# First norm's modulation in two halves of the channels; later modulation, constants and the context's projections moved

## The chip, the core and the metric

The kernel runs on one core of a Trainium2 chip. The metric is the device time of one execution in microseconds (us), as the median of three runs. The core has five engines that work side by side, each through its own instructions in order: TensorE (PE: matmuls and transposes), VectorE (DVE), ScalarE (ACT), GpSimd (POOL) and SyncE (SP), whose work here is to issue DMA transfers.

## What is computed

One call runs a hybrid block and then two layers of a second block, on 512 tokens of width 1024 with a context of 256 tokens. This case touches only the front of the first block:

```python
mod = silu(c) @ w_mod + b_mod            # 6 x 1024: shift, scale, gate, shift, scale, gate
hx  = rms_norm(x, g_mix) * (1 + scale) + shift
hc  = rms_norm(ctx, g_mix) * (1 + scale_c) + shift_c
px  = split_columns(hx @ w_in)           # q, k, v, gate of retention, windows, neighbourhoods
pc  = hc @ w_in[:, the k and v columns]  # the context's keys and values
ya  = retention_mixer(px, pc, log_sigmoid(decay_logit), ...)
mx  = gated_merge(px['gates'], ya, yb, yc, ...)
```

`c` and the context's `c_ctx` give two rows of modulation each time. After the merge come a mixture of 16 experts and the second block, whose two layers have modulations `mod_w[l]` of their own.

## The kernel before

Activations stay on chip with the channels on the partitions: `hx` is eight pairs of tiles of 128 channels x 512 tokens, `hc` the same with 256 tokens. A float32 product is made of three matmuls: `mm3` (L404 to L406) multiplies high by high, low by high and high by low part, and `w` loads a 512 KB weight piece through SP's queue (L412) and splits it on ScalarE (L395) and VectorE (L391). One projection is 24 matmuls: 8 tiles of channels x 3.

A modulation is `modblock` (L471): pieces of 128 x 1024 weights (512 KB, L470) come through SP's queue, and each gives two matmuls with the two silu columns as stationary operand, written to two groups of 32 rows. Then ScalarE copies the rows (L477), PE transposes them (L480), VectorE adds the bias. `modblock` is a generator that stops after each piece, and `pace`, `alt` and `weave` set how often the surrounding code takes one. For the block at hand:

- `block1_mixer` first drains the whole shift and scale modulation (`wmod0`, 16 pieces, seven buffers), computes `A1` from the scales, and norms all eight channel tiles (`normmod`, L569) to `hx`.
- Then it runs the first half of the retention's projections, `ret_proj(0)`: two q and two k projections with their rotation, the context's keys `kc`, the values `v`, the context's values `vc`, two gates. Between them `pace` takes pieces of the remaining modulations from the chain `mods` (`wmod1`, `wmod2`, then 24 pieces of the second block's layer 1, three buffers). `PACE` holds how much work lies between pieces.
- `ret_consts` (L734 on) computes the decay tables from the log-sigmoid; `ret_attn(0)` is woven with `ret_proj(1)` and `mods`, `ret_attn(1)` with output gates and `mods`; what is left of `mods` is then drained.
- Much later the third `merge` and `outproj` are alternated with the modulation of layer 0 of the second block (24 pieces, six buffers), one piece after each step of the merge and two after each step of `outproj`.

The text above sets priorities; a list scheduler then orders the instructions of each engine, and gives out buffers as they come free. Constants are loaded by `const` when first named, on GpSimd's queue.

## Time and profile before

| | |
|---|---|
| three runs | 2779.96, 2788.20, 2794.11 us; median 2788.20 |
| the profiled execution's own time | 2794.44 us |
| its span | 2792.6 us |
| mean granted clock of TensorE | 0.973 of 2.4 GHz |
| busy share of PE, DVE, ACT, POOL | 94%, 56%, 44%, 6% |
| bytes moved | 537.68 MB, mean 193 GB/s |

The span runs from the first to the last instruction; the time lies 1.8 us around it. A busy share is a mean over the whole span. The granted clock is the share of full clock that TensorE was given in a stretch: 1.00 is 2.4 GHz, 0.50 is 1.2 GHz. DMA share is the mean busy share of the core's 16 DMA engines.

### The profile page before, as it was taken

To read this page: it belongs to the slowest core of one execution; us is meant where nothing else is said; L and a number is where in the kernel's file an instruction comes from. 1 tells how busy PE (TensorE), PEld (TensorE's weight loads), DVE (VectorE), ACT (ScalarE), POOL (GpSimd) and SP (SyncE) were. 2 spreads that over 40 slices of the span, in tenths; PEclk is the share of its full clock that TensorE was granted. 3 is DMA by queue.
4 is the path that set the end of the run, shared out by engine and by line. 5 is a ranking of instruction groups with operands and counts; after the bars stand their busy time and mean duration, and the time that the engine had idled before them with its cause. 6 is when DMAs were issued, how large, how long until landed. Compare 5 with 4: busy or idle time off the path is not lost. (4 is left out here: it accounts for less than half of the span.)

```text
span 2792.6 us, 41759 instructions
## 1 busy us (share of the span) xinstructions
PE 2625.3 (94%) x16372; PEld 1859.9 (67%) x16372; DVE 1569.8 (56%) x2957; ACT 1230.6 (44%) x2159; POOL 161.0 (6%) x260
## 2 busy tenths in 40 slices
PE   6999999999958999999998899999999999999997
PEld 2666677887633566555654577777777777777776
DVE  3564677676441324456232656656866546766974
ACT  3333355444222224365222444545655645555652
POOL 1000001110001000000000000000010000000001
PEclk9899999999979999999999899999999999999998
DMA  8545424634879999988999332213354332114353
GB/s 287 177 164 191 146 85 161 209 120 156 298 283 325 340 380 356 335 297 300 352 366 372 126 106 83 77 51 136 118 186 135 128 123 84 62 39 140 117 177 114
DMA packets 167974, 537.68 MB, mean 193 GB/s; under 512 B 21272, under 2 KB 22376, under 8 KB 167776
## 3 DMA queue, kind: packets, MB, share of 16 engines
q1 hardware_dynamic: 138528, 460.40, 47.2%
q0 software_dynamic: 17152, 52.57, 5.8%
q10 hardware_dynamic: 12096, 22.03, 2.1%
q8 instruction: 129, 2.11, 0.3%
q14 instruction: 69, 0.57, 0.1%
HBM read 484.06 MB, written 48.76 MB: 191 GB/s over the span
## 5 line engine op out<-in xcount | busy, mean ns | idle before, releaser
L391 DVE TENSOR_TENSOR wl<-wr,wh 128x1024 fp32r<-128x1024 f32 x320 | 390.8, 1223 | 386.8 <-ACT wh L395 357.3
L395 ACT CAST wh<-wr 128x1024 fp32r<-128x1024 f32 x320 | 334.4, 1047 | 458.2 <-PE ps L405 348.6
L404 PE MATMUL ps<-hx,wh 128*128 128x512 f32 x1168 | 473.8, 406 | 5.8 <-ACT hx L569 5.1
L405 PE MATMUL ps<-hx,wh 128*128 128x512 f32 x1168 | 468.8, 402 | 0.1
L406 PE MATMUL ps<-hx,wl 128*128 128x512 f32 x1168 | 466.9, 400 | 0.0
L404 PEld LDWEIGHTS ps<-hx,wh 128*128 128x128 f32 x1168 | 221.8, 190 | 66.9 <-issue 13.2
L1307 PE MATMUL ps<-we,xe 128*64 128x512 f32 x1024 | 241.1, 615 | 18.1 <-DMA we<-in_wexp 18.0
L405 PEld LDWEIGHTS ps<-hx,wh 128*128 128x128 f32 x1168 | 221.6, 190 | 52.3 <-issue 8.4
L406 PEld LDWEIGHTS ps<-hx,wl 128*128 128x128 f32 x1168 | 221.7, 190 | 50.2 <-issue 3.3
L673 ACT ACTIVATE P<-ps,st 128x768 f32<-128x768 f32 (+3 forms) x144 | 111.1, 771 | 142.6 <-DVE st L669 107.7
L1307 PEld LDWEIGHTS ps<-we,xe 128*64 128x64 f32 x1024 | 76.0, 141 | 144.8 <-issue 118.4
L404 PE MATMUL ps<-hc,wh 128*128 128x256 f32 x496 | 144.1, 291 | 0.1
L406 PE MATMUL ps<-hc,wl 128*128 128x256 f32 x496 | 139.8, 282 | 0.5 <-DVE wl L391 0.5
L405 PE MATMUL ps<-hc,wh 128*128 128x256 f32 x496 | 140.3, 283 | 0.0
L667 DVE TENSOR_REDUCE st<-ps 128x1 f32<-128x768 f32 (+3 forms) x144 | 114.2, 793 | 38.1 <-PE ps L406 35.3
L1307 PE MATMUL ps<-we,hT 128*64 128x512 f32 x512 | 122.8, 626 | 10.4 <-DMA we<-in_wexp 8.2
L695 PE MATMUL ps<-c_ident,P 128*128 128x128 f32 x688 | 110.0, 278 | 5.3 <-ACT PT L698 3.5
L404 PEld LDWEIGHTS ps<-hc,wh 128*128 128x128 f32 x496 | 94.1, 190 | 19.5 <-issue 14.2
L695 PEld LDWEIGHTS ps<-c_ident,P 128*128 128x128 f32 x688 | 79.9, 140 | 39.8 <-ACT PT L698 13.4
L471 PE MATMUL ps<-wm,sc_cc 128*32 128x512 f32 x384 | 89.4, 647 | 15.9 <-DMA wm<-in_wmod 14.1
L698 ACT COPY PT<-ps 128x512 f32<-128x512 f32 x123 | 70.1, 586 | 72.6 <-PE ps L695 71.9
L405 PEld LDWEIGHTS ps<-hc,wh 128*128 128x128 f32 x496 | 94.0, 190 | 4.0 <-issue 3.5
(517 smaller groups left out, 5036.1 us busy)
## 6 DMA issues: line engine op xcount, KB each, us to landing
we<-in_wexp SPq DMA_DIRECT2D x384, 512.0 KB
wr<-in_win SPq DMA_DIRECT2D x240, 512.0 KB
wm<-in_wmod SPq DMA_DIRECT2D x48, 512.0 KB
wr<-in_wbr SPq DMA_DIRECT2D x48, 512.0 KB
dram<-th ACTq DMA_DIRECT2D x72, 256.0 KB
mth<-dram SPq DMA_DIRECT2D x72, 256.0 KB
wr<-in_wout SPq DMA_DIRECT2D x32, 512.0 KB
dram<-mth POOLq DMA_DIRECT2D x48, 256.0 KB, 3.1
```

The lines of the kernel that those rows point to most:

```text
L391: s.nc.vector.tensor_tensor(out, a, b, ALU.subtract)
L395: i = s.nc.scalar.copy(hi, src)
L404: t.matmul(out, a[0], b[0], start=start, stop=False)
L405: t.matmul(out, a[0], b[1], start=False, stop=False)
L406: t.matmul(out, a[1], b[0], start=False, stop=stop)
L471: nc.tensor.matmul(ps[32 * j:32 * j + 32, :], sc[:, k, :], w[:, j % 2 * 512:j % 2 * 512 + 512], start=k == 0, stop=k == 7)
L667: nc.vector.tensor_reduce(st[:, 0:1], sc[:, :n], AX.X, ALU.max)
L673: nc.scalar.activation(p[:, :n], sc[:, :n], AF.Exp, bias=st[:, 1:2], scale=scale, accum_out=st[:, 2:3])
L695: nc.tensor.transpose(tp[:, j:j + 128], blocks[(i + j) // 128], s.const("ident"))
L698: nc.scalar.copy(parts[i // 512][:, :m], tp[:, :m])
L1307: nc.tensor.matmul(ps[64 * e:64 * e + 64, :], stat[:, k, 64 * e:64 * e + 64], ws[h][e][:, kk * 512:kk * 512 + 512], start=k == 0, stop=k == 7)
```

## The change

Six things change. The host puts the columns of the shift and scale weights in another order, so that each of two blocks of 1024 columns holds shift and scale of four channel tiles. `block1_mixer` runs one modulation and one norm per half, with `x` multiplied by its reciprocal root mean square ahead of both. `modblock` takes its pieces in pairs: two transfers issued, the second piece's first, then four matmuls, then one stop. The chain `mods` is no longer taken between the first four projections nor, by the program's text, in the rest of `ret_proj(0)`; `PACE` is (0, 3.5, 3.5), and `outproj` takes one pair per step. In `ret_proj` the context's keys and values come last. Five constants, 576 KB in all, are loaded when the windows' stage begins.

```diff
+    half = np.concatenate([np.arange(s, s + 512) for s in (0, 1024, 512, 1536)])
+    wm, bm = f["w_mod"][0], f["b_mod"][0]
+    for n, a in enumerate(_modchunks(wm[:, half[:1024]]) + _modchunks(wm[:, half[1024:]]) + _modchunks(wm[:, 2048:])):
...
-    o["bmod"] = _cols(f["b_mod"][0])
+    o["bmod"] = _cols(np.concatenate([bm[half], bm[2048:]]))
...
+    def const(s, name, late=False):
+            i = s.nc.gpsimd.dma_start(t, a)
+            if late:
+                s.late(i)
...
-        for k in range(8):
-            for j in range(nj):
-                if j % 2 == 0:
-                    w = s.wp.tile([128, 1024], F32, name=s.uid("wr"), tag="wraw", bufs=NRAW) if big is None else \
-                        big.tile([128, 1024], F32, name=s.uid("wm"), tag="wbig", bufs=s.nbig)
-                    nc.sync.dma_start(w, src[k][:, j * 512:j * 512 + 1024])
-                nc.tensor.matmul(ps[32 * j:32 * j + 32, :], sc[:, k, :], w[:, j % 2 * 512:j % 2 * 512 + 512],
-                                 start=k == 0, stop=k == 7)
-                if j % 2:
-                    yield 0.9
+        parts = [(k, j) for k in range(8) for j in range(0, nj, 2)]
+        for i in range(0, len(parts), 2):
+            ws = []
+            for k, j in parts[i:i + 2][::-1]:
+                w = big.tile([128, 1024], F32, name=s.uid("wm"), tag="wbig", bufs=s.nbig)
+                nc.sync.dma_start(w, src[k][:, j * 512:j * 512 + 1024])
+                ws.insert(0, w)
+            for (k, j), w in zip(parts[i:i + 2], ws):
+                for e in range(2):
+                    nc.tensor.matmul(ps[32 * (j + e):32 * (j + e) + 32, :], sc[:, k, :], w[:, e * 512:e * 512 + 512],
+                                     start=k == 0, stop=k == 7)
+            yield 1.8
...
+    def normmod_x(s, x, k, a, b):
+
+        nc = s.nc
+        h = s.T(nm="nf")
+        nc.vector.tensor_scalar(h, x, a, b, ALU.mult, ALU.add)
+        hi, lo = s.TT(512, "hx", "hx")
+        nc.scalar.activation(hi, x, AF.Identity, bias=b, scale=a)
+        s.sub(lo, h, hi.bitcast(F32))
+        return hi, lo
...
-        for j in range(2):
-            kt = s.T(F32R, "kc", "pj")
-            ps = s.proj(win[c0 + 2 + j], s.hc, 256)
-            kc.append(s.split(ps[:, :256], kt[:, :256], kt[:, 256:]))
-            yield 2.6
...
-        yield from s.vproj(src, s.hc, 256, put(vc, "vc"))
         for j in range(2):
             gs.append(s.gate_silu(s.proj(win[c0 + 6 + j], s.hx), 512))
             yield 5.2
+        for j in range(2):
+            kt = s.T(F32R, "kc", "pj")
+            ps = s.proj(win[c0 + 2 + j], s.hc, 256)
+            kc.append(s.split(ps[:, :256], kt[:, :256], kt[:, 256:]))
+            yield 2.6
+        yield from s.vproj(src, s.hc, 256, put(vc, "vc"))
...
         rx = s.rstd_sb(s.sqsum(x, 512), D, 512)
+        for k in range(8):
+            nc.vector.tensor_tensor(x[k], x[k], rx, ALU.mult)
+        A1, B1 = [s.cp.tile([128, 2, 8], F32, name=n) for n in ("A1", "B1")]
+        s.hx = []
         with s.pool("bigA") as big:
             s.nbig = 7
-            drain(s.modblock(sc, s.d["wmod0"], 2048, mod, bm, 0, big))
-        A1 = s.cp.tile([128, 2, 8], F32, name="A1")
-        for v in range(2):
-            nc.vector.scalar_tensor_tensor(A1[:, v, :], mod[:, v, 8:16], 1.0, s.const("gmix"), ALU.add, ALU.mult)
-        s.hx = s.normmod(x, 512, A1[:, 0, :], mod[:, 0, 0:8], lambda: s.TT(512, "hx", "hx"), rx)
+            for hf in range(2):
+                c, o = 8 * hf, slice(4 * hf, 4 * hf + 4)
+                drain(s.modblock(sc, s.d[f"wmod{hf}"], 1024, mod, bm, c, big))
+                nc.vector.scalar_tensor_tensor(A1[:, :, o], mod[:, :, c + 4:c + 8], 1.0, gm2[:, :, o], ALU.add, ALU.mult)
+                nc.vector.tensor_copy(B1[:, :, o], mod[:, :, c:c + 4])
+                for k in range(4 * hf, 4 * hf + 4):
+                    s.hx.append(s.normmod_x(x[k], k, A1[:, 0, k:k + 1], B1[:, 0, k:k + 1]))
...
-            mods = itertools.chain(s.modblock(sc, s.d["wmod1"], 2048, mod, bm, 16, mr, bk[0]),
-                                   s.modblock(sc, s.d["wmod2"], 2048, mod, bm, 32, mr, bk[1]),
+            mods = itertools.chain(s.modblock(sc, s.d["wmod2"], 2048, mod, bm, 16, mr, bk[0]),
+                                   s.modblock(sc, s.d["wmod3"], 2048, mod, bm, 32, mr, bk[1]),
...
-                next(mods)
-            s.hc = s.normmod(c, 256, A1[:, 1, :], mod[:, 1, 0:8], lambda: s.TT(256, "hc", "hc"), rc)
-            drain(pace(g, mods, PACE[0]))
+            s.hc = s.normmod(c, 256, A1[:, 1, :], B1[:, 1, :], lambda: s.TT(256, "hc", "hc"), rc)
+            drain(g)
...
+            for n in ("ropem", "wrt", "cum", "pedge512", "pedge256"):
+                s.const(n, True)
...
-        drain(alt(s.outproj(hl, s.d["wout"], 512, put), mods, 2))
+        drain(alt(s.outproj(hl, s.d["wout"], 512, put), mods, 1))
...
-PACE = (2, 2.5, 2.5)
+PACE = (0, 3.5, 3.5)
```

`sub` of `normmod_x` is a subtraction on VectorE; in it ScalarE writes the high part and VectorE the shifted value and the low part.

How the instructions of PE move is seen at three places. `ps` are sums in PSUM, `wm` modulation pieces, `hx` and `hc` the normed inputs, `wh` and `wl` the two parts of a split weight piece, `qk` rotated queries and keys; the number is the buffer's in the program.

First place: PE between the first modulation and the first projection. Before:

```order
L471 MATMUL ps_153<-wm_210,sc_cc 32x512 x2
L471 MATMUL ps_153<-wm_214,sc_cc 32x512 x2
L480 MATMUL ps_220<-c_ident,mrow_218 128x128 x4
L404 MATMUL ps_302<-hx_235,wh_298 128x512
L404 MATMUL ps_375<-hx_235,wh_371 128x512
L405 MATMUL ps_302<-hx_236,wh_298 128x512
L405 MATMUL ps_375<-hx_236,wh_371 128x512
L471 MATMUL ps_289<-wm_411,sc_cc 32x512 x2
L471 MATMUL ps_289<-wm_457,sc_cc 32x512 x2
```

There two projections (`ps_302`, `ps_375`) begin behind the last transposes, and pieces of the next modulation follow. After, the end of the second half's pieces and what follows:

```order
L478 MATMUL ps_236<-wm_263,sc_cc 32x512 x2
L478 MATMUL ps_236<-wm_261,sc_cc 32x512 x2
L408 MATMUL ps_326<-hx_214,wh_322 128x512
L409 MATMUL ps_326<-hx_215,wh_322 128x512
L486 MATMUL ps_271<-c_ident,mrow_269 128x64 x4
L410 MATMUL ps_326<-hx_214,wl_323 128x512
L408 MATMUL ps_326<-hx_220,wh_322 128x512
L409 MATMUL ps_326<-hx_221,wh_322 128x512
L410 MATMUL ps_326<-hx_220,wl_323 128x512
```

Before, the whole modulation and its transposes (L480) stand ahead of the first projection matmul. After, the first half's transposes (L486, not shown) stand ahead of the second half's eight pieces, and the second half's transposes stand behind the first two projection matmuls; the projection's first twelve matmuls use the first half's channels.

Second place: PE behind the fourth projection (`ps_467` before, `ps_483` after). Before:

```order
L406 MATMUL ps_467<-hx_277,wl_464 128x512
L471 MATMUL ps_289<-wm_646,sc_cc 32x512
L471 MATMUL ps_289<-wm_689,sc_cc 32x512 x2
L471 MATMUL ps_289<-wm_719,sc_cc 32x512 x2
L497 MATMUL ps_515<-ones,sq_346 128x1 x2
L471 MATMUL ps_289<-wm_723,sc_cc 32x512 x2
L533 MATMUL ps_521<-c_ident,rs_518 128x128 x2
L471 MATMUL ps_289<-wm_754,sc_cc 32x512 x2
L471 MATMUL ps_289<-wm_784,sc_cc 32x512 x2
L471 MATMUL ps_289<-wm_827,sc_cc 32x512 x2
L471 MATMUL ps_289<-wm_831,sc_cc 32x512 x2
L404 MATMUL ps_581<-hc_528,wh_577 128x256
```

Here modulation pieces and the context's norm fill PE's queue up to the context's keys (`ps_581`). After:

```order
L408 MATMUL ps_483<-hx_300,wh_479 128x512
L409 MATMUL ps_483<-hx_301,wh_479 128x512
L410 MATMUL ps_483<-hx_300,wl_480 128x512
L478 MATMUL ps_313<-wm_1024,sc_cc 32x512
L408 MATMUL ps_598<-wh_588,hx_214 128x256
L409 MATMUL ps_598<-wl_589,hx_214 128x256
L410 MATMUL ps_598<-wh_588,hx_215 128x256
```

Before, seven and a half pieces and the context's norm (L497, L533) stand between the fourth projection and the next; in all, sixteen stand in `ret_proj(0)`. After, half a piece stands here, four and a half in `ret_proj(0)`, and the next rows are those of the values `v` (`ps_598`), with the context's last. Four pieces stand in a row behind the first score matmuls that follow:

```order
L408 MATMUL ps_1015<-qk_358,qk_431 128x512
L409 MATMUL ps_1015<-qk_359,qk_431 128x512
L410 MATMUL ps_1015<-qk_358,qk_432 128x512
L478 MATMUL ps_313<-wm_1152,sc_cc 32x512
L478 MATMUL ps_313<-wm_1150,sc_cc 32x512 x2
L478 MATMUL ps_313<-wm_1160,sc_cc 32x512 x2
L478 MATMUL ps_313<-wm_1158,sc_cc 32x512 x2
L849 MATMUL ps_966<-A_971,v_623 128x512
L408 MATMUL ps_1036<-hx_214,wh_1032 128x512
```

Behind them is the first product with the decay tables (`A_971`). None of these pieces stood here before: their matmuls moved down the queue from the projections.

Third place: the end of the 24 pieces of layer 1. Before:

```order
L471 MATMUL ps_289<-wm_2151,sc_cc_511 32x512 x2
L471 MATMUL ps_289<-wm_2155,sc_cc_511 32x512 x2
L471 MATMUL ps_289<-wm_2159,sc_cc_511 32x512 x2
L406 MATMUL ps_2220<-hx_247,wl_2217 128x512
L404 MATMUL ps_2220<-hx_253,wh_2216 128x512
L405 MATMUL ps_2220<-hx_254,wh_2216 128x512
L406 MATMUL ps_2220<-hx_253,wl_2217 128x512
L404 MATMUL ps_2220<-hx_259,wh_2216 128x512
L405 MATMUL ps_2220<-hx_260,wh_2216 128x512
L406 MATMUL ps_2220<-hx_259,wl_2217 128x512
L404 MATMUL ps_2220<-hx_265,wh_2216 128x512
L471 MATMUL ps_289<-wm_2163,sc_cc_511 32x512 x2
```

Three pieces stand together, then one at a time among projection matmuls. After:

```order
L478 MATMUL ps_313<-wm_2151,sc_cc_523 32x512 x2
L478 MATMUL ps_313<-wm_2149,sc_cc_523 32x512 x2
L486 MATMUL ps_2159<-c_ident,mrow_2157 128x128 x4
L478 MATMUL ps_313<-wm_2177,sc_cc_523 32x512 x2
L478 MATMUL ps_313<-wm_2175,sc_cc_523 32x512 x2
L478 MATMUL ps_313<-wm_2185,sc_cc_523 32x512 x2
L478 MATMUL ps_313<-wm_2183,sc_cc_523 32x512 x2
L478 MATMUL ps_313<-wm_2193,sc_cc_523 32x512 x2
L478 MATMUL ps_313<-wm_2191,sc_cc_523 32x512 x2
L478 MATMUL ps_313<-wm_2201,sc_cc_523 32x512 x2
L478 MATMUL ps_313<-wm_2199,sc_cc_523 32x512 x2
L486 MATMUL ps_2209<-c_ident,mrow_2207 128x64 x4
```

Before, five of the last eight pieces stand one by one among projection matmuls. After, the last eight, in four pairs, follow each other and the transposes with no other matmul between.

## Rows read from the trace of the kernel before

**Rows 1.** Windows: us, busy PE, PEld, DVE, ACT, POOL, PEclk, DMA share, GB/s

```profile
16.00:38.26 22.26, 17.23 (x69) 2.99 (x67) 0.35 (x2) 1.26 (x4) 2.84 (x6) 1.00 1.01 377
...
75.90:93.40 17.50, 10.87 (x38) 2.15 (x37) 16.43 (x35) 8.22 (x16) 0.00 (x0) 0.64 0.69 241
93.40:133.75 40.35, 40.35 (x256) 34.65 (x257) 13.56 (x34) 11.34 (x20) 0.00 (x0) 0.95 0.42 141
```

**Rows 2.** Timeline of PE, 36 to 134 us: start, us, instruction [idle before, releaser]

```profile
36.52 1.05 PE L471 MATMUL ps<-wm,sc_cc 128*32 128x512 f32 x4 [0.23 <-DMA wm<-in_wmod]
...
40.99 0.49 PE L404 MATMUL ps<-hx,wh 128*128 128x512 f32 x1 [2.07 <-ACT hx L569]
...
133.52 0.39 PE L406 MATMUL ps<-hx,wl 128*128 128x512 f32 x1
```

**Rows 3.** Waits of PE, 0 to 120 us: total us, times, longest

```profile
PE ps L471 <- DMA wm<-in_wmod: 13.9, 16, 2.6
```

**Rows 4.** Waits of PE, 120 to 460 us

```profile
PE ps L471 <- DMA wm<-in_mw1b: 1.8, 2, 1.3
```

**Rows 5.** Timeline of PE, projections of 512 and of 256 columns

```profile
57.22 0.39 PE L404 MATMUL ps<-hx,wh 128*128 128x512 f32 x1
...
59.49 0.39 PE L405 MATMUL ps<-hx,wh 128*128 128x512 f32 x1
...
98.11 0.28 PE L404 MATMUL ps<-hc,wh 128*128 128x256 f32 x1
...
98.71 0.40 PE L405 MATMUL ps<-hc,wh 128*128 128x256 f32 x2
```

**Rows 6.** Timeline of PE, pieces among the merge's and outproj's matmuls

```profile
698.09 0.39 PE L406 MATMUL ps<-yn,wl 128*128 128x512 f32 x1
698.41 1.05 PE L471 MATMUL ps<-wm,sc_cc 128*32 128x512 f32 x4
699.39 0.50 PE L404 MATMUL ps<-yn,wh 128*128 128x512 f32 x1
...
702.34 1.05 PE L471 MATMUL ps<-wm,sc_cc 128*32 128x512 f32 x4
...
732.60 1.07 PE L471 MATMUL ps<-wm,sc_cc 128*32 128x512 f32 x8
```

**Rows 7.** Timelines of SP's queue and of PE: pieces from issue to use

```profile
44.61 2.73 SPq L470 DMA_DIRECT2D wm<-in_wmod  x3
...
296.52 0.33 SPq L470 DMA_DIRECT2D wm<-in_mw1b  x1
...
48.33 1.05 PE L471 MATMUL ps<-wm,sc_cc 128*32 128x512 f32 x4 [1.36 <-DMA wm<-in_wmod]
...
300.66 1.05 PE L471 MATMUL ps<-wm,sc_cc 128*32 128x512 f32 x4 [0.41 <-DMA wm<-in_mw1b]
...
303.95 1.05 PE L471 MATMUL ps<-wm,sc_cc 128*32 128x512 f32 x4 [1.35 <-DMA wm<-in_mw1b]
```

**Rows 8.** Timeline of PE and a window: waits and the clock behind them

```profile
876.11 6.13 PE L1307 MATMUL ps<-we,hT 128*64 128x512 f32 x20 [4.14 <-DMA we<-in_wexp]
...
876.00:879.50 3.50, 3.39 (x8) 1.00 (x10) 0.00 (x0) 0.00 (x0) 0.00 (x0) 0.51 0.12 48
...
91.44 1.92 PE L471 MATMUL ps<-wm,sc_cc 128*32 128x512 f32 x4 [1.99 <-DMA wm<-in_wmod]
```

**Rows 9.** Timeline of ACT, then DVE's first product with the decay (summary of L832)

```profile
128.73 0.21 ACT L734 ACTIVATE ls<-c_lgt 128x8 f32<-128x8 f32 x1
...
L832 DVE SCALAR_TENSOR_TENSOR A<-ps,G x8: 628/685/694, 139.7 to 190.0; 128x512 f32<-128x512 f32 x8
```

**Rows 10.** Windows of the merge and the output projection

```profile
680.00:698.00 18.00, 18.00 (x99) 14.42 (x98) 4.82 (x7) 6.67 (x12) 0.00 (x0) 1.00 0.80 289
698.00:730.00 32.00, 32.00 (x132) 18.98 (x131) 19.61 (x27) 8.87 (x12) 2.12 (x4) 1.00 0.90 306
730.00:760.00 30.00, 30.00 (x144) 20.47 (x143) 11.57 (x13) 7.36 (x9) 2.17 (x4) 1.00 0.90 325
```

More of the change, by code (lines that the diff above doesn't have):

```diff
@@ L149, in prep @@
     o["cc"] = np.ascontiguousarray(np.stack([_cols(f["c"][0]), _cols(f["c_ctx"])], axis=-1))
-    m = _modchunks(f["w_mod"][0])
-    for n, a in enumerate(m):
+    half = np.concatenate([np.arange(s, s + 512) for s in (0, 1024, 512, 1536)])
+    wm, bm = f["w_mod"][0], f["b_mod"][0]
+    for n, a in enumerate(_modchunks(wm[:, half[:1024]]) + _modchunks(wm[:, half[1024:]]) + _modchunks(wm[:, 2048:])):
         o[f"wmod{n}"] = a
-    o["bmod"] = _cols(f["b_mod"][0])
+    o["bmod"] = _cols(np.concatenate([bm[half], bm[2048:]]))
     o["gmix"] = _cols(f["g_mix"][0])
@@ L368, in sc @@
         return s.P1("sc", 1536)
-    def const(s, name):
+    def const(s, name, late=False):
         if name not in s.cache:
@@ L373, in const @@
             t = s.cp.tile(list(a.shape), a.dtype, name="c_" + name)
-            s.load(t, a)
+            i = s.nc.gpsimd.dma_start(t, a)
+            if late:
+                s.late(i)
             s.cache[name] = t
@@ L1095, in block1_mixer @@
         bm = s.const("bmod")
+        gm2 = s.cp.tile([128, 2, 8], F32, name="gm2")
+        for v in range(2):
+            nc.vector.tensor_copy(gm2[:, v, :], s.const("gmix"))
         x = s.loadx("xT", 512, "pj")
         rx = s.rstd_sb(s.sqsum(x, 512), D, 512)
+        for k in range(8):
+            nc.vector.tensor_tensor(x[k], x[k], rx, ALU.mult)
+        A1, B1 = [s.cp.tile([128, 2, 8], F32, name=n) for n in ("A1", "B1")]
+        s.hx = []
         with s.pool("bigA") as big:
             s.nbig = 7
-            drain(s.modblock(sc, s.d["wmod0"], 2048, mod, bm, 0, big))
-        A1 = s.cp.tile([128, 2, 8], F32, name="A1")
-        for v in range(2):
-            nc.vector.scalar_tensor_tensor(A1[:, v, :], mod[:, v, 8:16], 1.0, s.const("gmix"), ALU.add, ALU.mult)
-        s.hx = s.normmod(x, 512, A1[:, 0, :], mod[:, 0, 0:8], lambda: s.TT(512, "hx", "hx"), rx)
+            for hf in range(2):
[5 more added lines that the diff above has]
+                    s.hx.append(s.normmod_x(x[k], k, A1[:, 0, k:k + 1], B1[:, 0, k:k + 1]))
         md, gd = s.dram([8, 128, 512]), s.dram([24, 128, 512])
```

## Prediction

> **What bounds the kernel now.** I read the page's busy shares first: TensorE (PE) is busy for 94% of the span, so a change pays where PE waits or where its clock is halved, and hardly elsewhere. The share is a mean over stages, so I went on to the windows. Three stretches matter [rows 1]. From 16.0 to 38.3 us the DMA share is 1.01 at 377 GB/s: the first modulation streams its sixteen 512 KB pieces as fast as they come, and PE follows it. From 75.9 to 93.4 us PE is busy for only 10.87 of 17.50 us at a mean clock of 0.64. From 93.4 to 133.75 us PE is busy throughout. Then the timeline of PE [rows 2]: the first modulation's last piece ends at 36.52 + 1.05 = 37.57 us, the first projection matmul starts at 40.99 us, and the last matmul of the first retention projections starts at 133.52 us and ends its stretch at 133.75 us. So this front part takes 133.75 - 37.57 = 96.2 us. The list of PE's waits up to 120 us puts 13.9 us on modulation pieces still in flight [rows 3], and from 120 to 460 us only 1.8 us on the last ones [rows 4]. What the front costs without waits follows from two steady intervals [rows 5]: ten 512-column matmuls between 57.22 and 59.49 us give 0.227 us each, five 256-column ones between 98.11 and 98.71 us give 0.12 us each.
>
> **The change part by part.** All sums are made against the profiled execution, 2794.4 us (span 2792.6 and 1.8 us around it); it lies 6.2 us above the median of the three runs, 2788.2.
>
> *Front.* By the code and the order there are 144 matmuls of 512 columns and 192 of 256 columns in the first retention projections: 144 x 0.227 + 192 x 0.12 = 32.7 + 23.0 = 55.7 us. Before, sixteen later modulation pieces stood among them; after, four and a half. A piece put into a stream of projections costs what lies between the projection matmul ahead of it and the one behind, less that one's own interval: 699.39 - 698.09 - 0.23 = 1.07 us, with a slower restart 1.2 us [rows 6]. A group of eight modulation matmuls (two pieces on different columns) has the same busy time, 1.07 against 1.05 us [rows 6]. Two and a half pairs and their restarts: 4 us, with other small work 6 us. For the start I take 3 us: the first half's norm is done while the second half's pieces stream, so the first matmul no longer waits for hx, but the second half's norm has only the first half's twelve matmuls (12 x 0.227 = 2.7 us) as cover, and a short dip of the clock may follow. 55.7 + 6 + 3 = 64.7 us, so the front loses 96.2 - 64.7 = 31.5 us (28 to 34). What is late next there is PE itself. The halves do not bring the first modulation's end forward: the same sixteen pieces still come at the DMA's rate, its last pair runs 1.05 us longer because its last-landing piece is needed first, and the deferred constants (576 KB, 0.59 MB) free 0.59 MB at 377 GB/s = 1.6 us. I count these at nothing. Deferred, the constants go down GpSimd's queue much later, where DMA has room; a gain or loss of 1.6 us is the bound.
>
> *New waits of PE for pieces.* Pieces are now taken in pairs, but still from three buffers, and SyncE (SP) issues its queue in order. By the buffers' release, the piece of a pair that PE needs first goes into the buffer which the pair before it frees with its own first piece. So its transfer can't start before PE has done that one, and PE must have other work for as long as the transfer takes. The trace has two pieces that PE waited for, from issue to use: 296.52 to 300.66 us, 4.14 us, and 44.61 (the first of three issues) to 48.33 us, 3.72 us [rows 7]. I take 3.9 us. In most places projections of 5 us and more stand between pairs. Not so in four: after the first score matmuls, where two pairs stand together (3.7 us of wait, which also hides the late decay chain, below); one pair at the ends of the second modulation's pieces (3.0); the last pair but four (1.8); and the final four pairs of the 1024-wide modulation, which now run with nothing in between (the last order above). There the first of the four has its neighbour's second piece and four transposes as cover, 3.9 - 1.0 - 0.7 = 2.2 us of wait; the three others only a second piece, 3.9 - 0.85 = 3.05 us each; and the transposes at the end wait some 0.8 us for ScalarE's copy: 2.2 + 9.2 + 0.8 = 12.2 us. Sum of waits: 3.7 + 3.0 + 1.8 + 12.2 = 20.7 us; the 2.0 us of such waits that stood in this stretch go (1.8 of them in [rows 4]), so +18.7 us (12 to 22). Behind these waiting matmuls stand the second retention and the later projections on PE, and nothing passes them. The pieces that left the front are run here too, but as pairs they cost per pair about what a single cost: +0.6 us.
>
> *Clock.* In this trace a wait of 4.14 us before 876.11 us is followed by 3.5 us at 0.51 [rows 8], 1.7 us lost; and behind a wait of 1.99 us at 91.44 us, one of several in a row, four modulation matmuls took 1.92 us [rows 8] in place of 1.05, the clock's lower level, 1.2 instead of 2.4 GHz. I charge 1.7 us for each of the two waits of 3 us and more, and for the final four pairs 4 x (1.92 - 1.05) + about 2.5 us behind them = 6 us: +9.4 us (0 to 11). On the Trainium skill, page "TensorE: Matmul & The Clock Gate", section "HAM oscillation — how this bites in real kernels": it warns that short bursts of matmuls, each waiting for its own transfer, keep falling back to the low clock. It speaks against this change, and the row at 91.44 us agrees; without it the clock term would be nothing, with it as here.
>
> *Decay chain.* ScalarE's first step is at 128.73 us and the first product with it at 139.7 us [rows 9], 11 us, before under gates and scores. It now starts after the context's projections, which come last; about 8 us of score and projection matmuls cover it, the rest falls into the 3.7 us above. Alone it would cost 3 us; beside that wait nothing.
>
> *Merge.* The third merge and output projection now take pieces in pairs, so sixteen groups of matmuls (eight single pieces, then eight pairs) become twelve: -4 x 1.2 = -4.8 us. But the merge now needs sixteen pieces where it took eight: 8 x 0.52 MB at 377 GB/s = 11.1 us more of DMA in stretches whose shares are 0.80, 0.90 and 0.90 [rows 10]. Up to 730 us that leaves 18 x 0.20 + 32 x 0.10 = 6.8 us free; up to 4.3 us could show as waits. Six buffers hold three pairs ahead, so I take 2 us (0 to 7, and more with the clock, see the third rival): -2.8 us (-5 to +6).
>
> Sum: -31.5 + 18.7 + 0.6 + 9.4 - 2.8 = -5.6 us. From 2794.4 that is 2788.8, and with the profile's 6.2 us over the median taken off, 2782.6; I say 2783.
>
> **The rivals.** *First: the waits are short and the clock stays up.* For it: a piece that streams is 0.52 MB at 377 GB/s = 1.4 us in the first modulation [rows 1], and single waits of 1 to 2 us in the trace (1.35 at 303.95 [rows 7]) left the clock alone. Against it: a buffer's release, an issue and a landing follow each other here, none streaming. If a transfer takes 2.6 us, each of about seven chained waits is 1.3 us shorter: waits +10.3, clock +2: -31.5 + 10.3 + 0.6 + 2 - 2.8 = -21.4 us, 2767 us. The Trainium skill, page "DMA: Bandwidth & Descriptors", section "Anatomy of one DMA — SWDGE (gpsimd) path", gives about 2.0 us and the bytes at 436 GB/s, by estimate 3.2 us for a piece; by it the seven waits would be some 5 us shorter together, 2778 us, but both rows are longer.
>
> *Second: the change doesn't bring what the halves say.* The first modulation stays at the DMA's rate whichever way it is cut, so the first projection moves only from 40.99 to about 38 us, and all the rest comes from the pieces' removal. If the second half's norm is late (2.1 us of wait for hx as before, and a dip in the clock of 1.7 us), the front gains 28 us: 2786 us. It lies inside the forecast's range.
>
> *Third, the other side: the merge becomes bound by transfers.* Eight pairs wait for a piece each once DMA is full: 4.3 us of missing transfer and the latency behind it, say 1.2 us a pair = 9.6 us, and 1.7 us of low clock behind most of them, 11 us: +20.6 in place of the +2 that I took: 2783 + 18.6 = 2802. It decides once a pair needs its transfer within less than the 7.9 us that two pairs ahead give (two groups stand 3.93 us apart, 698.41 and the next at 702.34 [rows 6]). Against it: before, PE has no gap there at a share of 0.90.
>
> **How the numbers follow.** The forecast, 2783, has a chance of 0.50, the second rival 0.14, the first 0.27, the third 0.09. The term bounds added up give -31.5 - 2.5 + 12 + 0.6 + 0 - 5 = -26.4 at one end and -28 + 22 + 0.6 + 11 + 6 = +11.6 at the other, 2762 and 2800. All ends at once are unlikely on the low side, so the range is 2766 to 2800. Half a per cent, 14 us, is about what a measurement of this kernel tells from no change: faster means under 2774, slower over 2802. Most of the first rival and a small part of the forecast lie below 2774: 0.28; the upper part of the third above 2802: 0.08; the rest 0.64.
>
> **What would show it.** In the profile after: the first retention projections end near 102 us without a stretch of idle PE; the waits list between 100 and 300 us names modulation pieces with some 20 us, 12 of them in the last four pairs; the granted clock falls to 0.5 at their end; PE has no gap in the merge around 660 to 720 us. If the projections end after 106 us, the front was sized wrong; if the waits are under 12 us, the transfer time; if the merge shows waits, the third rival holds.

## The result: one per cent slower

The changed kernel takes 2815.97 us (median of seven runs, 2808.21 to 2825.39), the kernel before 2784.63 us in the runs beside it: a ratio of 1.0098 (95% interval 1.0075 to 1.0121). I had forecast 2783 us with a range of 2766 to 2800. The direction is wrong and the time lies outside the range.

The profiled execution of the changed kernel took 2821.3 us, its span is 2819.5 us, 26.9 us over the span before. To see where they arise I cut both timelines at the starts of the same matmuls: the first score matmul of the retention, the context's first matmul in the windows' stage, a point 2.4 us into the third merge, and the first sum of squares behind the output projection. The windows of PE between these cuts, before and then after (columns as in rows 1):

```profile
37.57:135.26 97.69, 84.61 (x419) 57.67 (x418) 56.64 (x116) 36.41 (x62) 0.64 (x2) 0.86 0.57 195
135.26:318.60 183.34, 181.35 (x858) 118.88 (x857) 97.75 (x137) 61.77 (x83) 2.12 (x4) 1.00 0.53 180
318.60:698.00 379.40, 375.84 (x2234) 300.77 (x2234) 267.15 (x576) 188.07 (x381) 37.21 (x68) 1.00 0.42 142
698.00:786.20 88.20, 87.52 (x384) 54.95 (x382) 41.47 (x57) 23.32 (x31) 6.45 (x12) 1.00 0.76 265
```

```profile
37.60:106.56 68.96, 63.29 (x371) 51.86 (x367) 44.55 (x76) 31.24 (x52) 1.07 (x2) 1.00 0.53 179
106.56:334.19 227.63, 197.12 (x913) 122.62 (x911) 104.36 (x170) 67.23 (x90) 4.77 (x9) 0.92 0.53 179
334.19:714.00 379.81, 376.46 (x2233) 302.29 (x2234) 264.22 (x574) 184.23 (x377) 37.40 (x68) 0.99 0.41 140
714.00:806.40 92.40, 84.76 (x382) 55.14 (x382) 43.30 (x62) 25.07 (x32) 6.47 (x12) 0.98 0.69 253
```

| stage | before, us | after, us | difference | forecast |
|---|---|---|---|---|
| up to the first score matmul | 135.3 | 106.6 | -28.7 | -31.5 |
| from there to the windows' stage | 183.3 | 227.6 | +44.3 | +28.7 |
| up to the third merge | 379.4 | 379.8 | +0.4 | 0 |
| merge and output projection | 88.2 | 92.4 | +4.2 | -2.8 |
| the rest of the span | 2006.4 | 2013.1 | +6.7 | 0 |

I take the last row for spread: the rest is the same work in all kernels here, and in the profiled runs of the experiments it takes between 1998.6 and 2016.0 us. The loss is in the second row. There PE's busy time has grown by 197.12 - 181.35 = 15.8 us at a clock of 0.92 in place of 1.00, and its idle time from 2.0 to 30.5 us. The waits of PE in this stretch after the change (total us, times, longest) answer to [rows 4]:

```profile
PE ps L478 <- DMA wm<-in_wmod: 11.4, 7, 4.6
PE ps L478 <- DMA wm<-in_mw1b: 7.7, 4, 2.0
PE ps L478 <- DMA wm<-in_mw1a: 4.4, 4, 2.5
PE ps L408 <- DVE r L742: 4.0, 1, 4.0
PE ps L486 <- ACT mrow L483: 2.1, 3, 0.7
PE ps L849 <- DVE A L847: 0.8, 1, 0.8
```

23.5 us are waits for modulation pieces, 6.9 us are waits for VectorE and ScalarE. Summed from start to start in PE's timeline, waits left out, the pieces' matmuls in this stretch took 28.2 us before and 37.9 us after, all the rest 153.2 and 159.2 us. The last pairs, on PE's timeline after the change, against [rows 7] before:

```profile
304.75 1.93 PE L478 MATMUL ps<-wm,sc_cc 128*32 128x512 f32 x8 [2.54 <-DMA wm<-in_mw1a]
307.42 1.11 PE L486 MATMUL ps<-c_ident,mrow 128*128 128x128 f32 x4 [0.73 <-ACT mrow L483]
310.56 3.63 PE L478 MATMUL ps<-wm,sc_cc 128*32 128x512 f32 x8 [2.03 <-DMA wm<-in_mw1b]
316.06 3.63 PE L478 MATMUL ps<-wm,sc_cc 128*32 128x512 f32 x8 [1.87 <-DMA wm<-in_mw1b]
321.59 3.63 PE L478 MATMUL ps<-wm,sc_cc 128*32 128x512 f32 x8 [1.90 <-DMA wm<-in_mw1b]
327.12 1.91 PE L478 MATMUL ps<-wm,sc_cc 128*32 128x512 f32 x8 [1.91 <-DMA wm<-in_mw1b]
329.71 0.46 PE L486 MATMUL ps<-c_ident,mrow 64*128 64x64 f32 x4 [0.68 <-ACT mrow L483]
334.19 0.58 PE L408 MATMUL ps<-hc,wh 128*128 128x256 f32 x1 [4.01 <-DVE r L742]
```

Each pair comes 5.5 us after the one before it, three run at half the clock (3.63 against 1.91 us), and at the end PE waits 4 us for VectorE. The transfers are chained as forecast: SP issues the piece that the pair at 316.06 us needs first only when the pair at 310.56 us is done with its own first piece, and it lands 3.5 us later (SP's queue, and the DMA list for the window 312.40 to 313.00 with its us to landing):

```profile
312.52 0.33 SPq L474 DMA_DIRECT2D wm<-in_mw1b  x1
```

```profile
wm<-in_mw1b SPq DMA_DIRECT2D x1, 512.0 KB, 3.5
```

What VectorE did meanwhile:

```profile
308.94 0.16 DVE L1479 TENSOR_SCALAR vh<-c_vec 128x5 f32<-128x5 f32 x1
330.21 0.24 DVE L492 TENSOR_TENSOR mod<-ps,c_mb 128x8 f32<-128x8 f32 x2 [21.11 <-PE ps L486]
...
330.65 0.68 DVE L737 TENSOR_TENSOR r<-ps,pc 128x512 f32<-128x512 f32 x1
...
333.44 0.69 DVE L742 TENSOR_TENSOR r<-ps,pc 32x512 f32<-32x512 f32 x1
```

It stood for 21.11 us with the modulation's addition at the head of its queue. The rotation of the windows' keys, whose sums had lain ready since 302 us, came behind that.

### The profile page after: what moved, and what is told of

It reads as the page before. It is cut to its first block, busy times and chain, and to the rows that moved or that the text cites. A ratio compares the mean times of both kernels' runs of the same rounds, so it can differ in the third digit from the quotient of the medians.

```text
span 2819.5 us, 41801 instructions
## 1 busy us (share of the span) xinstructions
PE 2623.7 (93%) x16376; PEld 1864.5 (66%) x16376; DVE 1573.3 (56%) x2971; ACT 1231.8 (44%) x2160; POOL 159.9 (6%) x260
## 5 line engine op out<-in xcount | busy, mean ns | idle before, releaser
L399 ACT CAST wh<-wr 128x1024 fp32r<-128x1024 f32 x320 | 334.2, 1046 | 457.0 <-PE ps L409 322.3
L408 PEld LDWEIGHTS ps<-hc,wh 128*128 128x128 f32 x496 | 94.5, 191 | 21.8 <-issue 13.1
L478 PE MATMUL ps<-wm,sc_cc 128*32 128x512 f32 x384 | 77.9, 664 | 29.8 <-DMA wm<-in_wmod 17.7
L408 PE MATMUL ps<-mh,wh 128*128 128x512 f32 (+1 forms) x256 | 95.1, 371 | 2.1 <-ACT wh L399 2.1
```

Source lines behind the costliest of these rows:

```text
L399: i = s.nc.scalar.copy(hi, src)
L408: t.matmul(out, a[0], b[0], start=start, stop=False)
L478: nc.tensor.matmul(ps[32 * (j + e):32 * (j + e) + 32, :], sc[:, k, :], w[:, e * 512:e * 512 + 512], start=k == 0, stop=k == 7)
```

## The experiments

The theories, told apart below: A, pairs chained through three buffers cost transfers and clock behind the front; B and G, there are too many pieces in that stretch whatever their form; C, pieces in the front wait there instead; D, the halves are what brought the front its 28 us; E, what helps is where the pieces stand; F, the front waits for VectorE's two norms, of which the halves take off the first and the context's late place the second; H, the context's late place gains at the first score matmul only what is given back behind it.

**Order of issue within a pair.**

```diff
-            for k, j in parts[i:i + 2][::-1]:
-                ws.insert(0, w)
+            for k, j in parts[i:i + 2]:
+                ws.append(w)
```

> Changed kernel, but the two transfers of a pair are issued in the order of use. Theory A (the loss lies behind the first retention projections: pairs of pieces chained through three buffers, so that PE waits a whole transfer per pair and runs at the low clock): each transfer now has three pieces of lead in place of two, the last pairs no longer wait 2 us each, and 15 to 25 us come back: about 2796 us (2788 to 2803). Rival B (the order within a pair does not matter; the pieces that left the front are simply too many for the time that is left): no change, 2813 to 2819 us.

2810.2 us, a ratio of 1.0065 (1.0042 to 1.0089) to before. Only about 6 us come back by the medians, and the interval overlaps that of the change (1.0075 to 1.0121): neither theory's number. The stage from the first score matmul to the windows' shrinks from 227.6 to 220.0 us, but the wait for VectorE at its end grows to 6.3 us.

**Pairs in the front again.**

```diff
+                next(mods)
-            drain(g)
+            drain(pace(g, mods, PACE[0]))
-PACE = (0, 3.5, 3.5)
+PACE = (4, 3.5, 3.5)
```

> Changed kernel, but pairs of pieces are again taken between the first retention projections (PACE 4, 3.5, 3.5). Theory A: no pairs are left to be drained at the end (34 us there in the changed kernel for 10 us of work), while the front takes about six pairs more, 7 us: about 2790 us (2780 to 2798). Rival C (whatever is put into the front waits there for transfers, as before the change, at the low clock): the front gives back 15 us and more, 2800 us or above.

2784.7 us, 0.9983 (0.9968 to 0.9998): 31 us faster than the change as it was. The first score matmul comes at 111.1 in place of 106.6 us, so the front pays only 4.5 us for its pairs, and the context's first matmul in the windows moves from 334.2 to 305.7 us. Theory C falls.

**Single pieces in the merge.**

```diff
-        mods = itertools.chain(s.mods2(0, M[0], big), s.mods2g(0, M[0], big))
+        mods = itertools.chain(s.mods2(0, M[0], big, None, 1), s.mods2g(0, M[0], big, None, 1))
-        drain(alt(s.outproj(hl, s.d["wout"], 512, put), mods, 1))
+        drain(alt(s.outproj(hl, s.d["wout"], 512, put), mods, 2))
```

> Changed kernel, but in the third merge and the output projection the pieces are taken singly as before, one per step and then two. Theory A: the two 2.1 us waits for split weights there and the low clock behind them go, 4 to 8 us: about 2810 us. Rival: the loss in the merge is only shifted from the stages ahead of it, 2814 to 2818 us.

2808.3 us, 1.0069 (1.0049 to 1.0090). From the windows' stage to the end of the output projection this run takes 802.2 - 334.2 = 468.0 us, the changed kernel 472.2, the one before 467.6. So the 4.2 us are the pairs' here; the median's 8 us hold spread besides. In the changed kernel PE waits there for the splits of weights, not for pieces (PE's timeline, ScalarE's, a window, the timeline of SP's queue, and from the DMA list the us from that weight piece's issue to its landing):

```profile
737.28 0.50 PE L408 MATMUL ps<-yn,wh 128*128 128x512 f32 x1 [2.11 <-ACT wh L399]
...
749.17 0.50 PE L408 MATMUL ps<-mh,wh 128*128 128x512 f32 x1 [2.11 <-ACT wh L399]
```

```profile
747.55 0.62 ACT L399 CAST mh<-mth 128x512 fp32r<-128x512 f32 x1 [2.89 <-DVE mth L624]
748.08 1.99 ACT L399 CAST wh<-wr 128x1024 fp32r<-128x1024 f32 x2
```

```profile
716.00:748.00 32.00, 28.96 (x139) 16.75 (x137) 17.13 (x24) 5.73 (x9) 2.13 (x4) 0.95 0.98 363
```

```profile
720.11 1.08 SPq L474 DMA_DIRECT2D wm<-in_mw0a  x2
...
723.36 1.96 SPq L474 DMA_DIRECT2D wm<-in_mw0a  x2
725.58 0.37 SPq L416 DMA_DIRECT2D wr<-in_wbr  x1
```

```profile
wr<-in_wbr SPq DMA_DIRECT2D x1, 512.0 KB, 9.4
```

The DMA share is 0.98 where [rows 10] have 0.90, a weight piece (`wr`) is issued behind four modulation pieces and lands only 9.4 us later, at 735.0 us, and PE then waits for its split (L399). That is the first wait of 2.1 us. The second is not a late transfer: its weight piece is issued at 735.68 us and lands 8.4 us later, at 744.1, but its split starts only at 748.08 us, because in ScalarE's queue it stands behind a tile of the merge (`mh`) that waits for VectorE. A third wait stands at the stage's end: the pairs are used up early, their last transposes start at 793.97 us, and PE then stands idle before the sum of squares, where before the change the last modulation matmuls and their transposes ran (782.32 to 786.23 us):

```profile
PE ps L503 <- DVE sq L551: 2.9, 1, 2.9
```

PE's busy time in the stage fell by 2.8 us, from 87.52 to 84.76, and its idle time rose by 7.0 us.

**The halves alone**, on the kernel before: the reordered columns and the two norms of the change, everything else as before.

> The kernel before with the first edit alone: shift and scale in two halves of the channels, two norms; pieces single, PACE, constants and context as before. Theory A: the first projection starts some 2 us earlier, the pieces among the projections still wait: 2 to 6 us faster than before, about 2780 us. Rival D (the halves are what brought the changed kernel's 28 us in the front): about 2757 us.

2774.4 us, 0.9947 (0.9928 to 0.9967): 15 us under the kernel before in the runs beside it, where I had expected 2 to 6, and half of what theory D says. The first score matmul comes at 120.2 us. What the traces show behind it is VectorE. In the kernel before, the window of the first 15 us of projections and VectorE's groups from 38 to 54 us (busy us, mean ns of one | idle) are:

```profile
38.26:53.00 14.74, 8.98 (x26) 1.93 (x26) 13.42 (x22) 7.29 (x10) 0.00 (x0) 0.78 0.83 288
```

```profile
L570 DVE SCALAR_TENSOR_TENSOR hx<-nf,mod,hx 128x512 fp32r<-128x512 f32 x8 | 6.0, 748 | 0.0
L567 DVE SCALAR_TENSOR_TENSOR nf<-x,A,rb 128x512 f32<-128x512 f32 x8 | 5.8, 748 | 0.0
```

11.8 us of norm, ahead of the low parts of the first weights. With the halves VectorE is busy for 11.39 us while the pieces still stream, where it had 0.35 us before [rows 1]:

```profile
16.00:38.26 22.26, 19.02 (x77) 5.05 (x76) 11.39 (x28) 6.73 (x10) 1.83 (x4) 1.00 1.02 393
```

PE's waits for pieces in the front are shorter too (4.5 us against 9.6), though the pieces still stand there, and the granted clock from 36.00 us to the first score matmul is 0.94, where it was 0.86 from 37.57 us on.

**PE kept busy between the last pairs.**

```diff
+            if warm is not None and i + 2 < len(parts):
+                h = s.hx[0][0]
+                for _ in range(12):
+                    s.late(nc.tensor.matmul(warm, h[:, 0:128], h[:, 0:512], start=True, stop=True))
```

> Changed kernel, but behind each of the first three of the last four pairs stand twelve more projection-sized matmuls (2.7 us at the full clock) that write sums nobody reads. They lie inside the 3 us in which PE waits for the next transfer, so they keep PE busy. Theory A (the low clock is part of the price of these pairs): the pairs run in 1.9 instead of 3.6 us, the granted clock of that stretch rises to 1.00, and the context matmul behind them moves from 334.2 to about 328 us. Rival (the transfers set the period of 5.5 us, the clock hides in it): the same point stays at 333 to 336 us.

2812.6 us in its one execution. The context's matmul comes at 335.3 us: the rival's number. PE's timeline:

```profile
310.97 3.63 PE L478 MATMUL ps<-wm,sc_cc 128*32 128x512 f32 x8 [3.27 <-DMA wm<-in_mw1b]
314.53 3.72 PE L483 MATMUL ps<-hx 128*128 128x512 f32 x12
318.18 1.91 PE L478 MATMUL ps<-wm,sc_cc 128*32 128x512 f32 x8
320.02 3.06 PE L483 MATMUL ps<-hx 128*128 128x512 f32 x12
323.00 1.91 PE L478 MATMUL ps<-wm,sc_cc 128*32 128x512 f32 x8
324.84 3.06 PE L483 MATMUL ps<-hx 128*128 128x512 f32 x12
328.28 1.91 PE L478 MATMUL ps<-wm,sc_cc 128*32 128x512 f32 x8 [0.38 <-DMA wm<-in_mw1b]
```

The clock does rise from the second pair on (1.91 us), but nothing is gained: from the first pair to the last it is 17.3 us, 16.6 in the changed kernel. This does not say by itself that the low clock is free. The first interval is 7.2 us, the added matmuls running in part at the low clock too, and in the first two intervals PE no longer waits for a piece, so that the added work sets them; only the last pair waits for its transfer (0.38 us). What the run does show is how long the chain waits for a pair's first piece at the full clock: the next transfer is issued 319.27 - 318.18 = 1.09 us after the pair's start, where it was 312.52 - 310.56 = 1.96 us at half the clock.

```profile
319.27 0.33 SPq L474 DMA_DIRECT2D wm<-in_mw1b  x1
```

By estimate the low clock thus lengthens the chain by 0.87 us a pair, 2.6 us for three; the second piece of a pair runs while the next transfer is under way.

**VectorE not waiting for the last modulation.**

```diff
-            nc.vector.tensor_tensor(o, pv[:, 0:nj, :, v], b, ALU.add)
+            nc.vector.tensor_tensor(o, b if noadd else pv[:, 0:nj, :, v], b, ALU.add)
```

> Changed kernel, but VectorE does not read the transposed sums of the last modulation: layer 1's gates are the bias alone, so that much of the computation is left out. Theory A: VectorE stands with this addition at the head of its queue for the 21 us of the last pairs, and the rotation of the windows' keys behind it (3.5 us) then keeps PE waiting for 4.0 us; with nothing to wait for it is done early, and the context matmul moves from 334.2 to about 330 us. Rival (VectorE is only the last of several that PE waits for there): ScalarE's copy or a split weight takes its place, 333 us or later.

2813.6 us in its one execution. This run is some 4 us late from the start (its first projection matmul is at 41.87 us, 39.01 in the changed kernel, its first score matmul at 110.84), so the absolute number doesn't decide; the place itself does:

```profile
336.96 0.46 PE L486 MATMUL ps<-c_ident,mrow 64*128 64x64 f32 x4 [0.68 <-ACT mrow L483]
337.35 0.39 PE L408 MATMUL ps<-hc,wh 128*128 128x256 f32 x1
```

From the transposes to the context's matmul it is 0.4 us, where it was 334.19 - 329.71 = 4.5 us. The wait was VectorE's queue, and at this place nothing takes over. The stage as a whole gains less: it is 337.35 - 110.84 = 226.5 us, 1.1 us under the changed kernel's, as the waits for pieces ahead of it come to 28.5 us in place of 23.5. What the 4.0 us are worth by themselves stays open.

**Pieces held at their place**, in the kernel before and with the halves.

```diff
-                nc.tensor.matmul(ps[32 * j:32 * j + 32, :], ...
+                m = nc.tensor.matmul(ps[32 * j:32 * j + 32, :], ...
+                if hold:
+                    s.late(m)
```

> The kernel before, whole in its norm, but the matmuls of the first later modulation are kept at their place in the program's text, so the scheduler can't pull four and a half pieces ahead behind the first projection matmuls, nor seven and a half together in front of the context's. Theory E (the front's loss is where the pieces stand, not the norm's wait): the first score matmul moves from 135.3 to about 122 us, time 2777 us (2772 to 2782). Rival D (the halves are what gains): no change, 2785 to 2792 us.

> Both: the kernel before with the halves alone (as in the earlier run, 2774 us) and with the pieces of the first later modulation kept in place. Theory E: the first score matmul at about 115 us where it was 120.2, 2769 us (2765 to 2773). Rival (in the halves alone the pieces already stand well enough): 2774 us.

2787.0 us, 0.9993 (0.9974 to 1.0011), and 2780.4 us, 0.9979 (0.9964 to 0.9993): no gain before, and with the halves 6 us worse than without the hold. The first score matmul comes at 133.8 us (135.3 before), and with the halves at 124.8 (120.2 without the hold). Theory E falls, and PE's timeline in the kernel before with held pieces shows why:

```profile
49.66 0.80 PE L406 MATMUL ps<-hx,wl 128*128 128x512 f32 x1 [6.41 <-DVE wl L391]
...
80.64 0.66 PE L535 MATMUL ps<-c_ident,rs 128*128 128x128 f32 x2 [3.49 <-DVE rs L510]
84.85 0.80 PE L404 MATMUL ps<-hc,wh 128*128 128x256 f32 x2 [3.55 <-ACT hc L571]
```

Where the pieces had stood, PE now waits for the low parts of the weights and for the context's norm. The pieces, and their transfers, had been filling time that VectorE set.

**Halves, and the context last**; then the constants too. The edits are those of the change.

> The kernel before with two edits of the change: the halves, and the context's keys and values last in ret_proj. Pieces single, PACE and constants as before. Theory F (the front waits for VectorE: the norm of x, 12 us, and the norm of the context, 7 us, stand ahead of the splits that PE needs; the halves take the first under the streaming pieces, the context's place takes the second off): the context's norm is no longer waited for, the first score matmul comes at about 110 us where the halves alone have 120.2, and the time is 2767 us (2762 to 2772). Rival (the pieces, which filled these waits, then wait for their transfers instead): first score at 115 us or later, 2772 to 2780 us.

> As the kernel with halves and the context last, and the five constants deferred too. All theories: the constants (0.59 MB, 1.6 us of transfer) make no difference that can be measured, within 4 us of that kernel.

2784.1 us, 0.9989 (0.9977 to 1.0002), and 2784.1 us, 0.9988 (0.9972 to 1.0003). The constants are worth nothing that can be measured. With single pieces the context's place costs 10 us against the halves alone, so theory F misses: the first score matmul is 6.3 us earlier (113.9), the windows' stage 6.3 us later (308.5 against 302.2). PE's idle time from the first projection to the windows' stage is about the same (6.7 against 6.5 us); but it runs its pieces in 41 groups in place of 35, and from 107 to 150 us at a clock of 0.92, where the halves alone have 1.00. How these make up the loss is not shown.

**Single pieces throughout**, with PACE (0, 1.75, 1.75) and two per step of the output projection.

> Changed kernel with single pieces everywhere (PACE 0, 1.75, 1.75; two pieces per step of the output projection), but none by the text in the first retention projections. Theory A in its first form (the pairs are what costs): about 2785 us. Theory G (fifty-one pieces in the 200 us behind the front are the cost, one by one or in pairs, since three buffers give a piece every 4 us at most where single ones come in threes): 2797 to 2808 us, between the kernel with pairs in the order of use, 2810, less the 8 us of the merge, and that.

2804.5 us, 1.0049 (1.0030 to 1.0067; runs from 2791 to 2816), inside theory G's range. With none in the front, single pieces lose as well.

**Four buffers**, then with pairs in the front and single pieces in the merge, then with the context back in its old place.

```diff
-            s.nbig = 3
+            s.nbig = 4
-TAGS_A = tags(t=8, ...
+TAGS_A = tags(t=7, ...
```

> Changed kernel with four buffers for the later pieces in place of three (and seven scratch tiles in place of eight, for room). Theory A (the chain through three buffers is most of what the forecast lacked): a whole pair is ahead, no pair waits for a transfer that starts only with the pair before; the stage from the first score matmul to the context's first in the windows (227.6 us in the changed kernel) takes 205 us or less, time 2797 us (2790 to 2803). Theory G (too many pieces for what is left of the stage): 212 us or more, 2805 to 2812 us.

> As the run with pairs in the front (2785 us), with four buffers and single pieces in the merge as well. Theory A: 16.7 us of PE's idle time in the stage falls to about 8, the merge gives 3 us: 2773 us (2768 to 2779). Rival (the idle time there is VectorE's, for which the pieces wait): 2780 us or more.

> As the kernel before it in this list, with the context's keys and values back ahead of the values and gates. Theory H (the context's place gains at the first score matmul only what is given back behind it): the same or up to 6 us faster, 2767 to 2774 us. Rival (the context last is a gain): slower by 3 to 8 us.

Four buffers alone: 2798.5 us, 1.0034 (1.0018 to 1.0050), and the stage takes 316.8 - 109.2 = 207.6 us in place of 227.6. So 20 us of its 44 go with the fourth buffer, between the 205 us of theory A and the 212 of theory G; one scratch tile fewer is part of the edit too. Of the 24 us that stay, 17 are idle time of PE (19.1 us against 2.0): 11.6 us of waits for pieces, 6.0 of them at one place, 5.3 for VectorE's rotation and 2.2 for ScalarE's copies. The waits for pieces among them fit theory G. With the front and the merge as well: **2769.9 us, 0.9929 (0.9908 to 0.9949)**, faster than both kernels. Its interval overlaps that of the halves alone (0.9928 to 0.9967), so what the rest of the change adds to them even here is not clear of the noise. Its waits of PE from 36 to 340 us:

```profile
PE ps L849 <- DVE A L847: 7.5, 2, 4.2
PE ps L478 <- DMA wm<-in_wmod: 2.6, 2, 1.8
```

With the context back in place, 2779.8 us, 0.9962 (0.9948 to 0.9975): theory H falls, and the loss is larger than the 3 to 8 us of its rival. With pairs in the front the context's late place is a gain of 10 us; with the context first PE waits for its norm (waits of PE from 36 to 340 us):

```profile
PE ps L539 <- DVE rs L514: 5.2, 1, 5.2
PE ps L850 <- DVE A L848: 3.9, 2, 3.0
...
PE ps L408 <- DVE kc L395: 2.9, 1, 2.9
```

## Why the prediction was wrong

The step that failed is the sum behind the front: new waits +18.7, pieces +0.6, clock +9.4, together +28.7 us, measured +44.3. Of the 15.6 us that it lacked, idle time of PE is 9.8 (+28.5 in place of +18.7) and busy time 5.8 (+15.8 in place of +10.0). The merge, with its sign wrong, lacked 7.0 us more. Point by point:

- *Front, -31.5:* -28.7 measured. The size held, its reason only in part, which is luck. I put the lost time down to pieces in flight. The runs show the first score matmul at 135.3 us before, 120.2 with the halves, 113.9 with the context last as well, 113.3 with the constants deferred too, and 107.3 when, by the text, no pieces are taken in the front either. So the pieces' removal is about 6 us of it and the halves 15 (single executions; the first projections of the last four start up to 3 us apart). The held pieces (2787 us) show that keeping them from behind the first matmuls gains nothing by itself. In the second row of [rows 1] VectorE is busy for 16.43 of 17.50 us, and I read only PE's columns of it. My second rival, that the halves bring little and the pieces' removal the rest, is refuted by the halves alone, though its 28 us for the front are the nearer number.
- *Waits for pieces:* the mechanism held, a transfer that starts only with the pair before it. In the last pairs it takes 316.06 - 312.52 = 3.5 us from issue to use, against the 3.9 us that I took. The waits came to 23.5 us, where I had 19.9 without the copies. The last four pairs waited 7.7 us, not 11.4: the transfer is shorter, and at half the clock a pair's second piece covers more of it. The other waits that I had counted came to 4.6 us behind the first score matmuls (3.7), 3.3 at 160.73 us (3.0) and 2.5 before 304.75 us (1.8). The count of places was too small: "not so in four" leaves out eight shorter waits, 5.4 us together. By the formula of the Trainium skill, page "DMA: Bandwidth & Descriptors", section "Anatomy of one DMA — SWDGE (gpsimd) path", which it fits to transfers on GpSimd's path, a piece would take 3.2 us by estimate; the trace of these transfers, which SP issues, has the longer one again, 3.5 us.
- *What stands behind the wait:* I named PE's queue and forgot VectorE's. Its addition waits as long as the pieces do, and PE then waits 4.0 us for the rotation behind it; the run without that addition shows this wait gone. With ScalarE's three copies (2.1) and the decay table (0.8) that is 6.9 us, where I had 0.8.
- *Pieces, +0.6, and clock, +9.4:* the pieces' matmuls took 9.7 us more. 6.0 us of that is half the clock in the last pairs, 3 x (3.63 - 1.91) + 1.93 - 1.06. I had 6 us there too, but by luck: 0.87 us a pair and 2.5 us behind them. In the 1024-wide modulation both pieces of a pair write the same columns, so a pair takes 1.91 us and loses 1.72. I also added this to the waits, where it overlaps with them: by the estimate above only 2.6 us lengthen the chain. The other 3.7 us belong to the 12.5 pieces more that run here, for which I had 0.6. What falls on projections and scores is 6.0 us (159.2 against 153.2), and 3.4 us for that part was too little; the granted clock is 0.92 as a mean over the stage. The rule on the Trainium skill's page "TensorE: Matmul & The Clock Gate", section "HAM oscillation — how this bites in real kernels", that short bursts which each wait for a transfer fall back to the low clock and lose time by it, is borne out as to the clock and only in part as to its price: pairs that take 3.63 us at 1.2 GHz and 1.91 at 2.4 GHz lose 1.72 us each, of which by that estimate 0.87 counts.
- *Merge, -2.8:* +4.2. PE's busy time fell by 2.8 us, where I had 4.8 for the groups, and against the 2 us of waits that I had taken stand 7.0 us of idle time. My third rival is borne out in part: the DMA share went to 0.98, but no piece came late. One wait stands behind a weight piece that SP issued behind the pieces, one behind ScalarE's queue, and with the pieces used up early nothing covered VectorE's last squares.
- *First rival's sum:* seven waits shorter by 1.3 us each are 9.1 us and leave +9.6, not +10.3; its 2767 us would be 2766. The waits were not short, so nothing hangs on it.
- *Spread:* the profiled run of the changed kernel lies 5 us over its median; of the 31 us between the medians I can place 20 in the stages above, and the profiled rest of +6.7 us has no place. How much of the remainder is spread stays open.

## What to carry to other kernels

When a share is read per stage, read every engine's column. Here the matmul engine waited for transfers in stretches where VectorE was busy for 13.42 of 14.74 and 16.43 of 17.50 us; these waits filled VectorE's time, and with the pieces held back the next wait showed. When a wait is added, follow the queue of each engine that consumes its result, not only the one that waits. Count a buffer's release into the lead: with three buffers a pair's first piece had none, and one buffer more took 17 us off the same edit. And when one edit holds several changes, try each alone: no kernel here beats the halves by themselves clear of the noise.

## What the runs showed of the hardware

Two pieces on different columns cost PE what one costs (1.06 us for eight matmuls, 1.05 for four), while two on the same columns, as in the 1024-wide modulation, take 1.91 us. So pieces taken together on different columns save PE time where their transfers are there: from the first projection to the windows' stage the matmuls of the later pieces took 49.5 us before, and 33.7 us in the fastest kernel, summed from the starts in the timeline. Not all of this is the pairing: single pieces held in place, with the halves, took 41.8 us. And half the clock on work that waits for chained transfers costs less than its busy time says: of the 1.72 us that a last pair ran longer, by estimate 0.87 us stood ahead of the next transfer.
